# Softmax weights transposed by the tensor engine instead of by DMA, attention in rounds of three steps inside the projection gemm, and a fixed instruction order for the tensor engine in the first phase

## The chip, the cores and the metric

The kernel runs on one core of one Trainium2 chip. The metric is the device time of one execution in microseconds. In the texts PE is TensorE (the matmul engine), PEld its weight loads, DVE is VectorE, ACT is ScalarE, POOL is GpSimd and SP is SyncE, whose queue issues nearly all DMAs.

## The reference, cut to what matters

One layer of a decoder runs on 2048 prompt tokens and on 8 sample rows. The part that the change touches is the attention of the prompt. Its q, k and v come from one projection:

```python
def project_mixers(h, w_in, pos):
    z = h @ w_in                       # 1024 -> 2304 columns
    qa, ka, va, qb, kb, vb = jnp.split(z, points, axis=-1)
    ...
def banded_attention(q, k, v, window): # blocks of 128 queries, keys of the block and of the one before
    s = jnp.einsum('nbqhgd,nbkhd->nbhgqk', qb, kk) * scale
    s = jnp.where(valid[None, :, None, None], s, NEG)
    lse = jax.nn.logsumexp(s, axis=-1)
    p = jnp.exp(s - lse[..., None])
    o = jnp.einsum('nbhgqk,nbkhd->nbqhgd', p.astype(vv.dtype), vv)
...
def dilated_prompt(q, k, v):           # DIL_GROUPS = ((128, 1), (512, 4), (2048, 16))
    for w, d in DIL_GROUPS:
        ... banded_attention(to_res(q)[:, :, :, None], to_res(k), to_res(v), w // d)
    return combine_by_denominator(jnp.stack(outs), jnp.stack(lses), axis=0)
```

After it come the output projection, a cross-attention into 256 memory tokens, and a feed-forward network with a short convolution; all numbers are float32.

## The kernel before, in words

**Two phases.** The first computes the input projection, all the banded attention of the prompt and the keys and values of the memory tokens; the second runs output projection, cross-attention and feed-forward network in four chunks of 512 tokens. The change is in the first phase.

**The projection.** The 2304 columns of `w_in` are nine blocks of 256 (six of them, `COLS_A`, for mixer A, three, `COLS_B`, for mixer B), and the 16 tiles of 128 tokens are four groups. `ORDER` says which blocks of which group follow one another: first the six A blocks of groups 0, 1, 2 and 3, then the three B blocks of groups 3, 0, 1 and 2. For one block and one token tile `gemm_tile` (line 667) makes 24 matmuls of 256 columns: float32 is split into a high and a low part (`wh`, `wl`, `xh`, `xl`), and three products are summed over eight slices of the inner dimension. `evac_in` then turns queries and keys by their angles on DVE (`rope_to`) and stores the rows to DRAM. The last 16 tiles of the phase are those of the memory tokens (`mem_gemm`).

**The attention.** It is cut into 64 jobs (`Job`): 16 each of kinds `d1`, `d4`, `d16` and `b`; each job is a block of 128 queries with eight heads, worked on as two halves of four heads. The texts call a half a quad. There are 128 quads: 84 with two key blocks (the wide ones) and 44 with one (the narrow ones: all of `d16`, and the first blocks of the others). A quad passes three stages. `stage_a` computes the scores on PE into two PSUM banks (`se`, `so`), adds the mask and takes the maximum on DVE (line 556, four instructions), scales the maximum (line 559), and takes four exponentials on ACT (line 561). `stage_b` makes a float16 high part of the weights on ACT (line 569) and a low part on DVE (line 570) and lets one DMA transpose of the SP queue turn both into `pT` (line 572). `stage_c` multiplies with the values on PE (line 585) and copies the result on DVE (line 592). `job_prep` loads nothing: it transposes the job's queries and keys on PE into a bank of the PSUM pair `t` (lines 473 and 482), and ACT and DVE split them into high and low parts.

**What sets the order.** `attn_step` does one third of a round: scores of a quad, then the weights of an earlier quad, then the values of a still earlier one. `filler(n)` is called after every `gemm_tile` and makes two, three or four such steps, in a program order which a scheduler may then change: each engine's instructions are ordered by it at build time, and on the chip every engine works through its list in that order. In the second phase nothing of this changes.

Of the kernel before, what the change touches and what calls it, by code (L numbers as in the profile page):

```python
# [21 lines left out]
NS = 8  # L22
# [4 lines left out]
ST = 528  # L27
# [8 lines left out]
def tile_layer(ctx: ExitStack, tc: tile.TileContext, I, C, O):  # L36
# [32 lines left out]
    mm = nc.tensor.matmul  # L69
# [207 lines left out]
    nc.tensor.transpose(pv[:, 0:120], vrow, ident[:120, :120])  # L277
# [6 lines left out]
    def xprep(key, nxt=None):  # L284
# [3 lines left out]
        def norm():  # L288
            ss = sbL.tile([128, 1], F32, tag="ss", name="ss", bufs=3)
            junk = at_start("sm", 2) if key in range(4) else sbL.tile([128, 1024], F32, tag="xr", name="junk")  # L290
            act(out=junk[:rows], in_=x[:rows], func=ACTF.Square, accum_out=ss[:rows])
            r = sbL.tile([128, 1], F32, tag="r", name="r", bufs=18)
            rms_r(r[:rows], ss[:rows], 1.0 / D, 1, rows)
            rows_r[key] = r

        if key == "s":
            norm()
            pt = bank("t", 2)
            for k in range(8):
                nc.tensor.transpose(pt[:, k * NS:(k + 1) * NS], x[:NS, k * 128:(k + 1) * 128], ident[:NS, :NS])  # L300
# [13 lines left out]
        if key in (1, 2, 3):  # L314
            xr = at_start(*(("p2", 2), ("p2", 2), ("pT", 3))[key - 1]).rearrange("p (k t) -> p k t", k=8)
        else:
            xr = sbL.tile([128, 8, 128], F32, tag="xr", name="xr")
        for hf in range(2):
            pt = bank("t", 2)
            for k in range(4):  # L320
                kk = hf * 4 + k
                nc.tensor.transpose(pt[:, k * 128:(k + 1) * 128], x[:, kk * 128:(kk + 1) * 128], ident)
# [146 lines left out]
    def t_split(ins, hi, lo):  # L469
        pt = bank("t", 2)  # L470
        n = len(ins)
        for i, a in enumerate(ins):
            nc.tensor.transpose(pt[:, i * 128:(i + 1) * 128], a, ident)
# [4 lines left out]
    def t_copy(ins, out, eng="a"):  # L478
        pt = bank("t", 2)
        n = len(ins)  # L480
        for i, a in enumerate(ins):
            nc.tensor.transpose(pt[:, i * 128:(i + 1) * 128], a, ident)
        hi_of(out, pt[:, 0:n * 128].rearrange("p (k t) -> p k t", k=n), eng)

    def job_prep(job):
        job.full = job.kind == "d16" or (job.kind == "d4" and job.t == 0)
        if job.kind == "b":
            job.qh = sbR.tile([128, 4, 128], F32R, tag="qh", name="qh", bufs=2)
            job.ql = sbR.tile([128, 4, 128], F32R, tag="ql", name="ql", bufs=2)
            t_split([job.q[:, 128 * j:128 * j + 128] for j in range(4)], job.qh, job.ql)  # L490
            rh, rl = ring("b")
            s = job.t % 2
            t_split([job.k], rh[:, s], rl[:, s])
            job.kh, job.kl = rh, rl
        else:
            if job.full:
                job.qh = sbR.tile([128, 4, 128], F32, tag="qh", name="qf", bufs=2)
                job.kh = sbR.tile([128, 2, 4, 128], F32, tag="kh", name="kf", bufs=1)
                t_copy([job.q[:, 128 * j:128 * j + 128] for j in range(4)], job.qh)
                t_copy([job.k[:, 128 * j:128 * j + 128] for j in range(4)], job.kh[:, 1], "v")  # L500
                job.slots, job.vs, job.mo = [1], [job.v3], None
                job.ost = sbR.tile([128, ST], F32, tag="ost", name="ost", bufs=5)
# [3 lines left out]
            t_split([job.q[:, 128 * j:128 * j + 128] for j in range(4)], job.qh, job.ql)  # L506
            if job.kind == "d1":
                rh, rl = ring("d1")
                s = job.t % 2
            else:  # L510
                rh = sbR.tile([128, 2, 4, 128], F32R, tag="kh", name="kh", bufs=1)
                rl = sbR.tile([128, 2, 4, 128], F32R, tag="kl", name="kl", bufs=1)
                s = 1
            t_split([job.k[:, 128 * j:128 * j + 128] for j in range(4)], rh[:, s], rl[:, s])
            job.kh, job.kl = rh, rl
            if job.kind == "d4" and job.t > 0:
                t_split([job.kp[:, 128 * j:128 * j + 128] for j in range(4)], rh[:, 0], rl[:, 0])
                vprev["d4"] = job.vp3

        v3 = job.v3  # L520
        first = job.kind == "d16" or job.t == 0
        if first:
            job.slots, job.vs, job.mo = [s], [v3], None
        else:
            pv3 = vprev[job.kind]
            if s == 1:
                job.slots, job.vs, job.mo = [0, 1], [pv3, v3], 0
            else:
                job.slots, job.vs, job.mo = [0, 1], [v3, pv3], 1
        if job.kind in ("d1", "b"):  # L530
            vprev[job.kind] = v3
        job.ost = sbR.tile([128, ST], F32, tag="ost", name="ost", bufs=5)

    def stage_a(job, i):
# [15 lines left out]
        sm = sbR.tile([128, 4, 256], F32, tag="sm", name="sm", bufs=2)  # L550
# [62 lines left out]
    quads = deque()  # L613
    loaded = deque()
    pipe = {"b": None}
    ready = deque([None] * 2)
# [3 lines left out]
    def attn_busy():  # L620
        return bool(jobs or loaded or quads or pipe["b"] or any(ready))

    def attn_step():
        if not attn_busy():
# [1132 lines left out]
```

## Time and profile before

| | us |
|---|---|
| median of 3 runs | 3235.93 |
| lowest and highest run | 3235.06, 3238.74 |
| the profiled execution, its own time | 3230.24 |
| its span, from first to last instruction | 3228.5 |
| first phase, to about | 1000 |
| second phase | about 2228 |

The profiled execution's own time is 1.7 us above its span, and 5.7 us below the median of the runs. The mean granted TensorE clock over the span is 0.984. The first phase ends where the windows stop showing attention, at about 1000 us.

### The profile page before, as it was taken

Reading aid. Unit: us, or ns where it says so; the run is one execution under the profiler, and the core shown is the slowest. Engines: PE = TensorE matmul, PEld = TensorE weight load, DVE = VectorE, ACT = ScalarE, POOL = GpSimd, SP = SyncE. Lnnn points to the kernel's source line nnn. Section 1 sums busy time; section 2 is a strip of 40 time slices with the busy share of each in tenths; the row PEclk is TensorE's granted clock in tenths of the full one; section 3 lists DMA queues with packets and bytes.
Section 4 is the critical chain, followed back from the end, with each engine's and each line's share of the span. In section 5 each row is a group of like instructions: output and inputs, shape, how many; then the busy total and the mean of one; then the engine's idle time right before and its main releaser. Section 6 shows DMA issues by size and latency. Waiting matters only on the chain.

```text
span 3228.5 us, 58044 instructions
## 1 busy us (share of the span) xinstructions
PE 3100.5 (96%) x22290; PEld 2713.9 (84%) x22290; DVE 2147.1 (67%) x4299; ACT 1417.1 (44%) x2793; POOL 1013.7 (31%) x959
## 2 busy tenths in 40 slices
PE   8999989889888999999999999999999999999999
PEld 8998888788877888888887778798877778999998
DVE  7687677787886667665567766555687665554544
ACT  3555654666665444223444333444433343432322
POOL 2711613224244046342205524320554332110102
PEclk9999999998899999999999999999999999999999
DMA  6899999999897346664525555453476445223231
GB/s 211 249 253 237 270 243 230 252 242 220 191 231 230 119 152 209 204 198 162 207 97 184 169 168 183 144 196 111 159 240 235 157 151 179 73 86 96 89 95 64
DMA packets 621837, 580.14 MB, mean 180 GB/s; under 512 B 264140, under 2 KB 554104, under 8 KB 620432
## 3 DMA queue, kind: packets, MB, share of 16 engines
q1 hardware_dynamic: 616808, 572.21, 60.6%
q10 hardware_dynamic: 4608, 4.20, 0.4%
q8 instruction: 175, 2.87, 0.4%
q14 instruction: 102, 0.84, 0.1%
q0 software_dynamic: 144, 0.03, 0.0%
HBM read 457.55 MB, written 136.66 MB: 184 GB/s over the span
## 4 chain that ended last, share of the span: by engine, by line
PE 64%; DVE 7%; DMA 7%; POOL 3%; issue 3%; ACT 2%; SPq 1%; POOLq 0%; DVEq 0%; ACTq 0%
PE g L863 18%; PE g L862 18%; PE g L864 18%; DMA pT<-p 4%; PE s L1358 1%; PE g L1398 1%; PE o L585 1%; DVE wl L120 1%; DVE p L570 1%; DVE sm L556 1%; DMA kx<-in_cache_mem_k_dram 1%; PE g L672 1%; PE g L674 1%; PE g L673 1%; DMA mrg<-o_d 1%
## 5 line engine op out<-in xcount | busy, mean ns | idle before, releaser
L120 DVE TENSOR_TENSOR wl<-wr,wh 128x1024 fp32r<-128x1024 f32 (+1 forms) x406 | 535.7, 1320 | 359.8 <-ACT wh L110 358.3
L110 ACT ACTIVATE wh<-wr 128x1024 fp32r<-128x1024 f32 (+1 forms) x444 | 460.8, 1040 | 674.5 <-PE g L864 382.7
L863 PE MATMUL g<-h,wl 128*128 128x512 f32 (+2 forms) x2080 | 729.5, 351 | 0.0
L862 PE MATMUL g<-h,wh 128*128 128x512 f32 (+2 forms) x2080 | 729.5, 351 | 0.0
L864 PE MATMUL g<-h,wh 128*128 128x512 f32 (+2 forms) x2080 | 725.1, 349 | 0.0
L862 PEld LDWEIGHTS g<-h,wh 128*128 128x128 f32 x2080 | 390.7, 188 | 58.6 <-issue 1.0
L864 PEld LDWEIGHTS g<-h,wh 128*128 128x128 f32 x2080 | 391.2, 188 | 55.2 <-issue 0.5
L863 PEld LDWEIGHTS g<-h,wl 128*128 128x128 f32 x2080 | 390.8, 188 | 54.9 <-issue 1.4
L672 PE MATMUL g<-wh,xh 128*128 128x256 f32 x1152 | 340.4, 296 | 1.1 <-ACT z L383 0.7
L674 PE MATMUL g<-wh,xl 128*128 128x256 f32 x1152 | 333.1, 289 | 0.3 <-DVE xl L120 0.3
L673 PE MATMUL g<-wl,xh 128*128 128x256 f32 x1152 | 331.8, 288 | 0.0
L862 PE MATMUL g<-act,wh 128*128 128x512 f32 (+2 forms) x880 | 310.4, 353 | 8.2 <-ACT act L110 5.7
L863 PE MATMUL g<-act,wl 128*128 128x512 f32 (+2 forms) x880 | 309.4, 352 | 0.0
L864 PE MATMUL g<-act,wh 128*128 128x512 f32 (+2 forms) x880 | 308.0, 351 | 0.0
L561 ACT ACTIVATE sm<-sm,ost 128x256 f32<-128x256 f32 (+1 forms) x512 | 234.8, 460 | 155.1 <-DVE ost L559 154.4
L892 POOL TENSOR_TENSOR sq<-sq 128x512 f32<-128x512 f32 (+1 forms) x83 | 125.2, 1508 | 484.2 <-ACT sq L887 451.3
L672 PEld LDWEIGHTS g<-wh,xh 128*128 128x128 f32 x1152 | 223.5, 194 | 6.4 <-ACT z L383 0.9
L674 PEld LDWEIGHTS g<-wh,xl 128*128 128x128 f32 x1152 | 222.9, 193 | 4.0 <-DVE xl L120 1.2
L673 PEld LDWEIGHTS g<-wl,xh 128*128 128x128 f32 x1152 | 223.3, 194 | 2.1 <-issue 0.2
L862 PE MATMUL g<-oT,wh 128*128 128x512 f32 (+2 forms) x608 | 216.1, 356 | 4.5 <-ACT oT L110 4.5
L863 PE MATMUL g<-oT,wl 128*128 128x512 f32 (+2 forms) x608 | 215.9, 356 | 0.0
L864 PE MATMUL g<-oT,wh 128*128 128x512 f32 (+2 forms) x608 | 211.6, 355 | 0.0
(353 smaller groups left out, 6084.2 us busy)
## 6 DMA issues: line engine op xcount, KB each, us to landing
wr<-in_w_up_dram SPq DMA_DIRECT2D x176, 512.0 KB
wr<-in_w_down_dram SPq DMA_DIRECT2D x80, 512.0 KB
out_dram<-in_cache_a_k_dram SPq DMA_DIRECT2D x32, 1023.5 KB
out_dram<-in_cache_a_v_dram SPq DMA_DIRECT2D x32, 1023.5 KB
wr<-in_w_in_dram SPq DMA_DIRECT2D x60, 512.0 KB
v<-va_d SPq DMA_DIRECT2D x60, 384.0 KB
wr<-in_w_out_dram SPq DMA_DIRECT2D x32, 512.0 KB
wr<-in_w_xq_dram SPq DMA_DIRECT2D x32, 512.0 KB
```

The source lines that it names most:

```text
L110: act(out=out, in_=in_, func=ACTF.Copy)
L120: e.tensor_tensor(out=out, in0=in_, in1=hi.bitcast(F32), op=ALU.subtract)
L556: vec.tensor_tensor_reduce(out=sm[:, x, 0:n], in0=S[e][:, u * n:(u + 1) * n], in1=m_, scale=1.0, scalar=-3e38, op0=ALU.add, op1=ALU.max, a ...
L561: act(out=sm[:, x, 0:n], in_=sm[:, x, 0:n], func=ACTF.Exp, scale=0.125, bias=nb[:, x:x + 1], accum_out=job.ost[:, 520 + 4 * i + x:521 + 4 ...
L570: vec.tensor_tensor(out=p2[:, 1], in0=sm[:, :, 0:n], in1=p2[:, 0], op=ALU.subtract)
L672: mm(p[:, 0:256], h[:, kt, :], wh[:, q, :], start=(kt == 0), stop=False)
L673: mm(p[:, 0:256], h[:, kt, :], wl[:, q, :], start=False, stop=False)
L674: mm(p[:, 0:256], l[:, kt, :], wh[:, q, :], start=False, stop=(kt == 7))
L862: mm(o, wh[:, q, c], pn[:, 0, a:b], start=st, stop=False)
L863: mm(o, wl[:, q, c], pn[:, 0, a:b], start=False, stop=False)
L864: mm(o, wh[:, q, c], pn[:, 1, a:b], start=False, stop=en)
L892: pl.tensor_tensor(out=acc[:, 0:self.ncol], in0=acc[:, 0:self.ncol], in1=sq[:, 0:self.ncol], op=ALU.add)
```

## The change

The change has three parts.

1. `stage_b` no longer makes `p2` and no longer issues a DMA. Each key block of a quad's weights (four heads, 128x128 float32 each) is transposed by four PE instructions into a bank of `t`; ACT copies the bank to the float16 high part and DVE subtracts to get the low part, both straight into `pT`.
2. A round is one `stage_a`, then `stage_c` and `stage_b` together, then a part of `job_prep` of the next job, which now returns a list of pieces (`queries`, `keys`, `before`). `gemm_tile` and `mem_gemm` call `filler(1)` between matmuls of one accumulation, so that the steps of a round stand between pieces of six, nine or twelve matmuls. The number of steps for each tile stays two, three or four. A quad's values follow its weights one round later, not two.
3. All matmuls and transposes of PE go through `mm` and `tr`, which in the first phase fix them to program order (`keep_in_program_order`). The scheduler still orders DVE, ACT, POOL and SP.

`sm` has four buffers, not two, and the first `x` tiles use them.

```diff
-    mm = nc.tensor.matmul
+    in_order = [True]
+
+    def pinned(ins):
+        return tc.keep_in_program_order(ins) if in_order[0] else ins
+
+    def mm(*args, **kw):
+        return pinned(nc.tensor.matmul(*args, **kw))
+
+    def tr(*args):
+        return pinned(nc.tensor.transpose(*args))
...
     def stage_b(job, i, sm):
 
-        n = 128 * len(job.slots)
-        p2 = sbR.tile([128, 2, 4, n], F16, tag="p2", name="p2", bufs=2)
-        act(out=p2[:, 0], in_=sm[:, :, 0:n], func=ACTF.Copy)
-        vec.tensor_tensor(out=p2[:, 1], in0=sm[:, :, 0:n], in1=p2[:, 0], op=ALU.subtract)
-        pT = sbR.tile([128, 16, 128], F16, tag="pT", name="pT", bufs=3)[:, 0:n // 16]
-        nc.sync.dma_start_transpose(out=pT, in_=p2.rearrange("p g x k -> p (g x k)"))
-        v = pT.rearrange("p (g x h) t -> p g h x t", g=2, x=4)
-        return v[:, 0], v[:, 1]
+        nh = len(job.slots)
+        pT = sbR.tile([128, 2, 2, 4, 128], F16, tag="pT", name="pT", bufs=3)
+        for hf in range(nh):
+            pt = bank("t", 2)
+            for x in range(4):
+                tr(pt[:, x * 128:(x + 1) * 128], sm[:, x, hf * 128:(hf + 1) * 128], ident)
+            v = pt.rearrange("p (x t) -> p x t", x=4)
+            act(out=pT[:, 0, hf], in_=v, func=ACTF.Copy)
+            vec.tensor_tensor(out=pT[:, 1, hf], in0=v, in1=pT[:, 0, hf], op=ALU.subtract)
+        return pT[:, 0], pT[:, 1]
...
         elif s == 1:
...
+            if pipe["b"]:
+                stage_c(*pipe["b"])
+            pipe["b"] = None
+            if pipe["a"]:
+                jb, i, sm = pipe["a"]
+                pipe["b"] = (jb, i, *stage_b(jb, i, sm))
+            pipe["a"] = pipe["n"]
         else:
...
+            begin_prep()
+            if cur[0] is not None:
+                if len(to_prep) > 1 and nxt[0] is not None and not hasattr(nxt[0], "qh"):
+                    to_prep.popleft()()
+            else:
+                while to_prep:
+                    to_prep.popleft()()
...
-    def gemm_tile(u, h, l):
+    def gemm_tile(u, h, l, steps=0):
         p = bankA("g")
         for kt in range(8):
             wh, wl = u[kt // 4]
             q = kt % 4
+            if kt * steps // 8 > (kt - 1) * steps // 8 and kt:
+                filler(1)
             mm(p[:, 0:256], h[:, kt, :], wh[:, q, :], start=(kt == 0), stop=False)
...
-                p = gemm_tile(u, *xT[tt])
+                p = gemm_tile(u, *xT[tt], 4 if j in COLS_B else 2 if oi < 3 else 3)
...
-                filler(4 if j in COLS_B else 2 if oi < 3 else 3)
+                filler(1)
```

How the instructions now stand is shown at one place, in the `b` jobs near the end of the projection. These are the rows of PE of the changed kernel: the weights of one quad are transposed from `sm_14140` into both banks of `t`, six matmuls of the projection follow, then the queries of the next job (`raw`) are transposed into `t_14345`, and three more matmuls of the projection follow.

```order
L78 MATMUL t_14323<-ident_81,sm_14140 128x128 x4
L78 MATMUL t_14330<-ident_81,sm_14140 128x128 x4
L75 MATMUL g_14273<-wh56_12755,xh_13108 128x256
L75 MATMUL g_14273<-wl56_12756,xh_13108 128x256
L75 MATMUL g_14273<-wh56_12755,xl_13109 128x256
L75 MATMUL g_14273<-wh56_12755,xh_13108 128x256
L75 MATMUL g_14273<-wl56_12756,xh_13108 128x256
L75 MATMUL g_14273<-wh56_12755,xl_13109 128x256
L78 MATMUL t_14345<-ident_81,raw_13865 128x128 x4
L75 MATMUL g_14273<-wh57_12761,xh_13108 128x256
L75 MATMUL g_14273<-wl57_12762,xh_13108 128x256
L75 MATMUL g_14273<-wh57_12761,xl_13109 128x256
```

Before, `sm` had no reader on PE; `t` has two banks, given out in turn, so `t_14345` is the bank of `t_14323`. After three more matmuls of the projection the scores of the next quad follow (`se_14364`, `so_14365`).

On ACT of the kernel before, a comparable place in the `b` jobs reads so: exponentials of a quad (line 561), its float16 copy (line 569), and the copies of queries and keys from PSUM between them.

```order
L561 ACTIVATE sm_14004,ost_13878<-sm_14004,ost_13878 128x256 x4
L110 ACTIVATE ringb0_12763<-t_14150 128x128
L569 ACTIVATE p2_14155<-sm_14004 128x1024
L561 ACTIVATE sm_14130,ost_13878<-sm_14130,ost_13878 128x256 x4
L598 ACTIVATE es_14540<-es_14540 128x8
L110 ACTIVATE qh_14341<-t_14343 128x512
L569 ACTIVATE p2_14260<-sm_14130 128x1024
L561 ACTIVATE sm_14249,ost_14154<-sm_14249,ost_14154 128x256 x4
```

On ACT of the changed kernel, at the place that PE's rows show, the order is this (`pT` is written from the two banks of `t`, `qh` is the next job's queries):

```order
L570 ACTIVATE sm_14262,ost_14233<-sm_14262,ost_14233 128x256 x4
L583 ACTIVATE pT_14322<-t_14323 128x512
L583 ACTIVATE pT_14322<-t_14330 128x512
L120 ACTIVATE qh_14343<-t_14345 128x512
L570 ACTIVATE sm_14378,ost_14233<-sm_14378,ost_14233 128x256 x4
L583 ACTIVATE pT_14454<-t_14455 128x512
L583 ACTIVATE pT_14454<-t_14462 128x512
```

What moved: the exponentials of a newer quad (`sm_14262`) now stand ahead of the copies out of `t` for an older quad (`sm_14140`, by PE's rows). Counted over ACT's whole list of the changed kernel, this is so for 106 of the 128 quads.

On DVE of the changed kernel, the same place: mask and maximum of the newer quad (line 565, from `se` and `so`), their scale (line 568), the copy of the values' result (line 603), and then the two subtractions out of `t` (line 584) for the older quad and the low part of the queries.

```order
L565 ISA sm_14262,mx_14263<-so_14249,mask_102 128x256
L565 ISA mx_14263 128x1
L568 TENSOR_SCALAR ost_14233<-mx_14263 128x4
L603 COPY ost_13975<-o_14280 128x2x2x64
L584 TENSOR_TENSOR pT_14322<-t_14323,pT_14322 128x512
L584 TENSOR_TENSOR pT_14322<-t_14330,pT_14322 128x512
L130 TENSOR_TENSOR ql_14344<-t_14345,qh_14343 128x512
L565 ISA sm_14378,mx_14379<-se_14364,mask_102 128x256
```

Before, the subtraction (line 570) read `sm` and `p2` in SBUF and held no PSUM bank; now the two of line 584 stand between a quad's maxima and the next quad's.

## Rows read from the trace of the kernel before

**Rows 1.** The page: busy time by engine; the chain of waits by line, 107:1000.

```profile
PE 3100.5 (96%) x22290; PEld 2713.9 (84%) x22290; DVE 2147.1 (67%) x4299; ACT 1417.1 (44%) x2793; POOL 1013.7 (31%) x959
...
by line: DMA pT<-p 13.0%; PE o L585 4.0%; issue 3.7%; DVE p L570 3.3%; DVE sm L556 3.3%; PE g L672 3.0%; PE g L674 2.8%; PE g L673 2.8%; PE se L548 2.6%; PE so L548 1.7%; DVE ost L559 1.3%; ACT sm L561 1.3%; ACT p L569 1.2%; DVE t L363 1.1%
```

**Rows 2.** Windows by stage: length, PE, PEld, DVE, ACT, POOL, clock, DMA share, GB/s.

```profile
107.00:221.20 114.20, 107.76 (x1186) 102.10 (x1185) 89.66 (x273) 67.03 (x185) 45.76 (x52) 0.98 0.98 260
221.20:357.30 136.10, 125.80 (x1486) 118.44 (x1483) 100.87 (x285) 78.60 (x199) 33.36 (x36) 0.95 0.99 249
357.30:501.40 144.10, 130.66 (x1620) 122.14 (x1618) 101.14 (x279) 79.19 (x195) 46.24 (x45) 0.98 1.04 251
501.40:665.30 163.90, 144.68 (x1598) 131.49 (x1597) 131.67 (x481) 97.28 (x324) 57.43 (x52) 0.96 0.98 241
665.30:770.00 104.70, 93.74 (x1140) 85.28 (x1138) 84.61 (x264) 68.24 (x178) 29.33 (x26) 0.92 1.05 234
770.00:875.00 105.00, 95.20 (x1202) 86.22 (x1200) 89.54 (x297) 69.59 (x199) 32.01 (x32) 0.92 0.83 191
875.00:1000.00 125.00, 101.39 (x1338) 92.22 (x1338) 102.24 (x282) 82.93 (x223) 58.71 (x40) 0.95 1.02 243
```

**Rows 3.** Waits from 107 to 1000 us: total, times, longest.

```profile
ACT p L569 <- DMA pT<-p: 54.1, 28, 7.8
...
PE o L585 <- DMA pT<-p: 43.1, 34, 2.8
```

**Rows 4.** DVE by line and shape, 107 to 1000 us: busy us, mean ns.

```profile
L570 DVE TENSOR_TENSOR p<-sm,p 128x1024 f16<-128x1024 f32 x84 | 119.8, 1426 | 36.4 <-ACT p L569 36.1
...
L559 DVE TENSOR_SCALAR ost<-mx 128x4 f32<-128x4 f32 x128 | 39.3, 307 | 0.8
L570 DVE TENSOR_TENSOR p<-sm,p 128x512 f16<-128x512 f32 x44 | 36.8, 837 | 21.6 <-ACT p L569 21.4
L120 DVE TENSOR_TENSOR ql<-t,qh 128x512 fp32r<-128x512 f32 x44 | 29.9, 680 | 2.1 <-ACT qh L110 2.1
L556 DVE CUSTOM_DVE_ANT_0 sm<-so,mask 128x128 f32<-128x128 f32 x88 | 21.9, 282 | 4.4 <-PE so L548 4.4
```

**Rows 5.** ACT by line and shape, 107 to 1000 us: busy us, mean ns.

```profile
L561 ACT ACTIVATE sm<-sm,ost 128x256 f32<-128x256 f32 x336 | 166.4, 497 | 100.8 <-DVE ost L559 100.3
...
L561 ACT ACTIVATE sm<-sm,ost 128x128 f32<-128x128 f32 x176 | 68.4, 390 | 54.3 <-DVE ost L559 54.0
...
L110 ACT ACTIVATE qh<-t 128x512 fp32r<-128x512 f32 x44 | 25.8, 587 | 20.5 <-PE t L473 14.2 <-DMA pT<-p 3.8 <-PE so L548 2.5
```

**Rows 6.** Timeline around 710 us, clock at full level: start us, duration us, what.

```profile
709.86 0.38 PE L548 MATMUL so<-kh,qh 64*128 64x256 f32 x1
...
710.45 0.40 PE L548 MATMUL so<-kh,ql 64*128 64x256 f32 x2
...
711.50 1.34 PE L585 MATMUL o<-v,pT 128*128 128x64 bf16 x40 [0.65 <-DMA pT<-p]
...
712.73 0.41 DVE L556 CUSTOM_DVE_ANT_0 sm<-se,mask 128x256 f32<-128x256 f32 x1
...
712.88 0.28 PE L672 MATMUL g<-wh,xh 128*128 128x256 f32 x1
...
713.00 0.28 PE L673 MATMUL g<-wl,xh 128*128 128x256 f32 x1
...
714.10 0.08 DVE L556 DVE_READ_ACCUMULATOR2_ANT mx<- 128x1 f32 x1
```

**Rows 7.** Timeline of the start: transposes, first projection matmul, load of the sample rows.

```profile
8.34 1.94 PE L322 MATMUL t<-ident,x 128*128 128x128 f32 x8 [1.10 <-DMA x<-in_x_prompt_dram]
...
16.52 0.56 PE L672 MATMUL g<-wh,xh 128*128 128x256 f32 x1
...
21.65 0.42 SPq L259 DMA_DIRECT2D x<-in_x_sample_dram  x1
...
23.13 1.03 PE L322 MATMUL t<-ident,x 128*128 128x128 f32 x8
```

More of the change, by code (lines that the diff above doesn't have):

```diff
@@ L276, in tile_layer @@
     pv = bankA("pv")
-    nc.tensor.transpose(pv[:, 0:120], vrow, ident[:120, :120])
+    tr(pv[:, 0:120], vrow, ident[:120, :120])
     vec.tensor_copy(out=vecs, in_=pv[:, 0:120])
@@ L289, in norm @@
             ss = sbL.tile([128, 1], F32, tag="ss", name="ss", bufs=3)
-            junk = at_start("sm", 2) if key in range(4) else sbL.tile([128, 1024], F32, tag="xr", name="junk")
+            junk = at_start("sm", 4) if key in range(4) else sbL.tile([128, 1024], F32, tag="xr", name="junk")
             act(out=junk[:rows], in_=x[:rows], func=ACTF.Square, accum_out=ss[:rows])
@@ L472, in t_split @@
         for i, a in enumerate(ins):
-            nc.tensor.transpose(pt[:, i * 128:(i + 1) * 128], a, ident)
+            tr(pt[:, i * 128:(i + 1) * 128], a, ident)
         v = pt[:, 0:n * 128].rearrange("p (k t) -> p k t", k=n)
@@ L481, in t_copy @@
         for i, a in enumerate(ins):
-            nc.tensor.transpose(pt[:, i * 128:(i + 1) * 128], a, ident)
+            tr(pt[:, i * 128:(i + 1) * 128], a, ident)
         hi_of(out, pt[:, 0:n * 128].rearrange("p (k t) -> p k t", k=n), eng)
@@ L486, in job_prep, with queries @@
         job.full = job.kind == "d16" or (job.kind == "d4" and job.t == 0)
[L487 to L495, printed above, removed]
+        cols = [slice(128 * j, 128 * j + 128) for j in range(4)]
+        def queries():
             if job.full:
                 job.qh = sbR.tile([128, 4, 128], F32, tag="qh", name="qf", bufs=2)
[L498 to L502, printed above, removed]
+                t_copy([job.q[:, c] for c in cols], job.qh)
                 return
@@ L505, in job_prep @@
             job.ql = sbR.tile([128, 4, 128], F32R, tag="ql", name="ql", bufs=2)
[L506 to L509, printed above, removed]
-            else:
[L511 to L529, printed above, removed]
@@ L534, in stage_a, with before @@
+        def before():
+            t_split([job.kp[:, c] for c in cols], job.kh[:, 0], job.kl[:, 0])
+        return [queries, keys] + ([before] if job.kind == "d4" and job.t > 0 else [])
     def stage_a(job, i):
@@ L612, in tile_layer @@
     jobs = deque()
-    quads = deque()
     loaded = deque()
-    pipe = {"b": None}
-    ready = deque([None] * 2)
+    to_prep = deque()
+    cur = [None, 0]
+    nxt = [None]
+    pipe = {"a": None, "b": None}
     sub = [0]
@@ L620, in attn_busy, with attn_left, fetch, begin_prep @@
     def attn_busy():
-        return bool(jobs or loaded or quads or pipe["b"] or any(ready))
+        return bool(jobs or loaded or to_prep or nxt[0] or cur[0] or pipe["a"] or pipe["b"])
+    def attn_left():
+        return [*jobs, *loaded] + [j for j in (nxt[0], cur[0]) if j]
+    def fetch():
+        while len(loaded) < 2 and jobs:
+            jb = jobs.popleft()
+            job_load(jb)
+            loaded.append(jb)
+    def begin_prep():
+        if nxt[0] is None and loaded:
+            nxt[0] = loaded.popleft()
+            to_prep.extend(job_prep(nxt[0]))
     def attn_step():
@@ L697, in mem_prep @@
         if t == 0:
-            while any(jb.kind != "b" for jb in [*jobs, *loaded, *(q[0] for q in quads)]):
+            while any(jb.kind != "b" for jb in attn_left()):
                 filler(1)
```

103 lines of the change are left out of this document (58 added, 45 removed).

## The prediction

> **What bounds the kernel now.** I read the page first. PE is busy for 96% of the span [rows 1], but that mixes two phases. In the windows by stage [rows 2] the second phase is absent because nothing in it changes; the first phase, from 107 to 1000 us, has PE at 81% to 94% busy, and the granted clock at 0.92 to 0.98, so some stretches ran at 1.2 GHz. DVE is at 70% to 85%, and the DMA share is about 1.0 in six of the seven stages: the queue is full. The chain of waits of this stretch says what the fullness costs: 13% of it, some 116 of 893 us, is the landing of the transposed weights `pT`, more than any engine's line has [rows 1]. The waits say who stands still for it: ACT 54 us before it may reuse `p2`, PE 43 us before the values [rows 3]. So the first phase is held by a transfer, and PE and DVE both have time to spare in it.
>
> **What goes.** All 128 DMA transposes, with their waits. Also the DVE subtractions of line 570, 119.8 + 36.8 = 157 us [rows 4]. These waits cannot be subtracted as they stand, since what follows them may wait for something else. That is what has to be worked out.
>
> **What comes on PE.** 84 wide quads have two key blocks and 44 have one, each block is four transposes: (168 + 44) x 4 = 848. Eight transposes took 1.03 us at full clock and 1.94 at half [rows 7]; without the drain of the last that is 0.11 us each, so 94 us at full clock. PE's idle time in the seven stages is 893 - 799 = 94 us, and low clock hides more, so they fit only if they fall into idle time.
>
> **What comes on DVE and ACT.** 212 subtractions from PSUM, of the shape that `ql` has (0.68 us, [rows 4]): 144 us, 12 less than before. 212 copies out of PSUM like that of `qh` (0.59 us, [rows 5]) take about what the old float16 copies took. Neither engine gets fuller.
>
> **A round, by occupancy of PE.** Line 672's matmuls start 0.12 us apart [rows 6]. A round with four steps to a tile has 18 of them: 2.2 us. Twelve scores run in pairs, 6 x 0.12 = 0.7. Values 1.2 (1.34 with its drain, [rows 6]). Weights 0.9, queries or keys 0.45. Some seven changes of operand kind at 0.09, by estimate, 0.6. Sum 6.0 us. With three steps to a tile 6.7, with two 8.15.
>
> **A round, by what waits for what.** Here the pinned order matters. `t` has two banks. In the rows of order, the weights take both, so the queries or keys of the same round need the first one back, and on PE everything behind them stands still: six matmuls and the next quad's scores. The bank comes back after its copy on ACT and its subtraction on DVE. On ACT that copy stands behind the four exponentials of the newer quad (106 of 128 quads). Those need that quad's maxima, and those its scores, which are this round's first step. So the round closes on itself: scores, from the first start to the last end 709.86 to 710.85, 0.99 [rows 6]; mask and maximum 712.73 to 714.18, 1.45 [rows 6]; scale 0.31 [rows 4]; exponentials 4 x 0.497 and a last read, 2.05 [rows 5]; copy 0.59 [rows 5]; subtraction 0.68 [rows 4]; four transposes 0.44; six matmuls 0.72; changes of operand kind 0.2; seven hand-overs between engines, 0.3 by estimate. Sum **7.7 us**, against 6.0 of occupancy. With three and two steps to a tile the piece before the scores is longer: 8.1 and 8.45. Behind a transpose of keys the scores also wait for the low half (copy 0.59 and subtraction 0.68 against about 1.2 us of cover); with the two transposes of a `d4` job that is more, on average 0.35 us a round for `d1` and `d4`.
>
> Narrow quads use one bank, so the loop through `t` opens. Their line on DVE and ACT is shorter, four maxima of 0.28, scale 0.31, four exponentials of 0.39, copy, subtraction, 4.3 us with overlap; occupancy is 4.55. Every second round the keys' copy (0.68, as `ql`) and the scores come behind it: 5.65. Mean 5.1.
>
> **The sum, by stage of [rows 2].** Rounds by the program's loops, after against before:
> 107 to 221: 10 narrow rounds x 6.7 (occupancy with two steps), 6 x 8.45, 32 transposes of `x` 3.5: 121 against 114, +7.
> 221 to 357: 16 x 8.8 + 3.5 = 144 against 136, +8.
> 357 to 501: 16 x 8.45, then some 162 matmuls without attention, 20: 155 against 144, +11.
> 501 to 665: 32 x 5.1 + 6 for the sample rows = 169 against 164, +5.
> 665 to 770: 16 x 8.05 = 129 against 105, +24.
> 770 to 875 (`b`, keys are one transpose): 16 x 7.6 = 121 against 105, +16.
> 875 to 1000: 16 x 7.6, 96 matmuls alone 11.5, merge 7: 140 against 125, +15.
> That is +86. The start: PE's first projection matmul, at 16.52, now stands behind the transposes of the sample rows, whose load was issued at 21.65 [rows 7]; that is 10 us later at most, and part of it is caught up because transposes are then behind it: +6 (bounds 0 and 14). Turning instructions stand between maxima and scale at about 71 places of DVE's new list, at about 0.3 us: +20 (bounds 0, if they fill a wait, and 40). In 22 of 128 quads ACT takes the copy first, about 0.6 us gained each: -14. In all **+98**, so a span of 3228.5 + 98 = 3326. The profiled execution's own time, 3230.24, is 5.7 under the median of 3235.93, and the span 7.4: **3334 us**. The seven hand-overs and the changes of kind are the widest estimates: at nothing the loop is 7.2, at double 8.2, 84 wide rounds x 0.5 = 42 either way. Own range 3280 to 3385.
>
> **Rivals.** *PE sets the pace (faster).* The loop does not close, because copies come earlier on the chip than in my hand-worked round, and each wide round takes its occupancy: 120 + 134 + 127 + 152 + 98 + 93 + 111 = 835 (the last two with 5.8 a round, since a `b` job's keys are one transpose) against 893, -58; with +6 for the start and some 6 of remaining stalls, 3190. For it: all of the 116 us of landing leave the chain. Against: the orders of PE, ACT and DVE above leave no other way round. It decides as soon as a wide round falls under some 6.6 us, which is what the stage 665 to 770 takes now (105 us for 16).
>
> The Trainium skill, page VectorE: DVE Perf Modes, section The three transpose paths, speaks for this rival: it gives 390 ns for a 128x128 transpose on TensorE and 1309 ns for the DMA's, in 2-byte numbers. The trace agrees that PE's are far cheaper (0.11 us apart against a chain of landings), but the page says nothing of what queues behind a PSUM bank.
>
> *The loop half closes.* Where the matmul pieces of other lengths let ACT run ahead, half the rounds take the loop and half occupancy: (98 - 46) / 2, about +26, 3262. Slower still.
>
> *Dear transposes.* If transposes let the clock fall, they cost 1.94 us for eight, twice as much [rows 7]: 848 x 0.11 = 93 us more, of which those of the weights stand under the exponentials and those in the loop, half of the rounds' PE part with them, do not: +60 on top, 3394. For it: the clock is already at 0.92 in two stages whose PE has gaps [rows 2]; against: it is 0.95 to 0.98 in the three stages to 501 us, which transpose `q` and `k` too and most of them also `x`.
>
> The Trainium skill, page TensorE: Matmul & The Clock Gate, Part 4: PE-mode transpose, speaks against the change in this way: it measured about 275 ns in one kernel's context, and says that transposes do not count as activity for the clock. By 275 ns the 848 would be 233 us, not 94. The trace disagrees on the price: eight in 1.03 us [rows 7].
>
> *It does not do what it says.* Landing of other transfers, not of `pT`, could be what fills the queue; the loads of `q`, `k` and values then keep the first phase at its length: 3236. Against: `pT` alone is named in both waits [rows 3].
>
> **Chances.** Loop as worked out 0.60, half closed 0.10, dear transposes 0.06, PE sets the pace 0.19, no change 0.05. So slower by over 0.2% 0.75, within 0.2% (6.5 us, about what a measurement of this kernel can tell from no change) 0.05, faster 0.20. The range for 8 in 10 leaves out the upper half of the dear transposes and a little over half of the fast case: 3195 to 3395.
>
> **What would show it.** In the profile after: no DMA transposes and a DMA share well under 1.0; 848 new PE instructions at about 0.11 us; wide rounds 7.5 to 8.5 us apart (start of scores to start of scores) with PE waiting for the DVE subtraction before the transposes of queries and keys, and ACT's copy out of `t` waiting not for PE but behind exponentials; first phase ending near 1100. I am wrong if wide rounds come at 6.6 us or less, or if PE's longest waits there are for something else than the bank.

## The result and the profile after

The changed kernel takes 3431.0 us (median of 4 runs, 3426.2 to 3435.6) against 3235.5 of the kernel before: a ratio of 1.0607, 95% interval 1.0584 to 1.063, some 195 us slower. The direction was forecast, the size was twice the forecast +98, and the time lies outside the range. The profiled execution has a span of 3428.0 us.

The page first, its line of PE and its line of the DMA share in 40 slices:

```profile
PE 3198.8 (93%) x23138; PEld 2799.2 (82%) x23138; DVE 2156.7 (63%) x4383; ACT 1427.8 (42%) x2877; POOL 976.7 (28%) x959
...
DMA  6755554664324353566463555545366545232331
```

848 instructions of PE are new, as counted, and the DMA share is near one half where it was full. Next the windows by stage, which answer to [rows 2]; the stages end where the projection's matmuls of the same stage end (us, PE, PEld, DVE, ACT, POOL, clock, DMA share, GB/s):

```profile
118.70:259.70 141.00, 123.13 (x1319) 115.48 (x1317) 93.06 (x285) 69.95 (x199) 35.86 (x46) 0.96 0.59 180
259.70:420.70 161.00, 139.01 (x1606) 128.83 (x1605) 110.44 (x300) 81.94 (x212) 29.31 (x36) 0.97 0.54 157
420.70:579.60 158.90, 138.47 (x1708) 128.35 (x1707) 97.76 (x287) 77.14 (x204) 36.19 (x44) 0.99 0.53 160
579.60:670.20 90.60, 76.05 (x825) 69.60 (x825) 61.78 (x235) 45.86 (x155) 23.57 (x19) 0.91 0.58 171
670.20:761.10 90.90, 82.17 (x914) 75.27 (x913) 68.95 (x256) 49.26 (x168) 32.79 (x34) 0.95 0.66 190
761.10:896.20 135.10, 105.00 (x1285) 94.04 (x1284) 87.63 (x273) 69.69 (x194) 23.03 (x23) 0.94 0.43 124
896.20:1033.00 136.80, 103.07 (x1259) 93.72 (x1257) 88.63 (x296) 67.12 (x205) 29.05 (x36) 0.88 0.30 90
1033.00:1195.00 162.00, 128.44 (x1498) 116.69 (x1496) 100.01 (x311) 88.97 (x247) 49.51 (x39) 0.88 0.38 120
...
118.70:1195.00 1076.30, 895.35 (x10397) 821.96 (x10395) 708.25 (x2237) 549.93 (x1581) 259.31 (x274) 0.94 0.49 146
```

The last line is all the stages in one window. The first phase ends at 1195, not 1100. No engine is full in these stages: PE is at 75% to 90%, DVE at 62% to 76%, DMA at 0.66 or less. In all PE is busy for 895 us and idle for 181; before, by the lines of [rows 2], it was busy for 799 and idle for 94. So of the 183 us by which these stages grew, 96 are work of PE, about what 848 transposes at 0.11 us come to, and 87 are idle time. Such a picture is one of waits, so the waits of PE come next (118 to 1195 us: us in total, times, longest):

```profile
PE t L78 <- DVE pT L584: 83.4, 58, 4.0
PE t L78 <- issue: 20.9, 13, 2.3
PE t L78 <- ACT mz L1657: 12.0, 8, 5.2
PE t L78 <- DMA srow<-in_state_conv_dram: 11.2, 1, 11.2
PE t L78 <- DMA raw<-qa_d: 8.4, 1, 8.4
PE se L75 <- DVE ringd L130: 7.9, 7, 2.2
PE t L78 <- ACT xr L333: 7.4, 5, 3.6
...
PE se L75 <- DVE kf L124: 7.1, 7, 2.8
```

The longest is the one forecast: transposes (line 78) that wait for DVE's subtraction of the weights (line 584) to return the bank. Around it stands a list of waits for other things: all rows of this view add up to 179 us, and 83 of them are the bank's. The 13 waits for which the profile names no releaser (`issue`, 20.9 us) stand at the same place, before transposes of the next job's `raw`, and may be the bank's too. The timeline shows one wide round with that wait, and ahead of it a wait of PE and two pairs of matmuls, one at either clock (start us, us, what):

```profile
801.08 0.71 PE L78 MATMUL t<-ident,raw 128*128 128x128 f32 x4 [2.26 <-issue]
...
801.81 0.42 PE L75 MATMUL g<-wl,xh 128*128 128x256 f32 x1
802.02 0.41 PE L75 MATMUL g<-wh,xl 128*128 128x256 f32 x1
...
803.01 0.58 PE L75 MATMUL se<-ringd,qh 64*128 64x256 f32 x1
...
808.10 0.28 PE L75 MATMUL g<-wl,xh 128*128 128x256 f32 x1
808.22 0.28 PE L75 MATMUL g<-wh,xl 128*128 128x256 f32 x1
...
811.75 0.38 PE L75 MATMUL se<-kh,qh 64*128 64x256 f32 x1
...
819.86 0.38 PE L75 MATMUL se<-kh,qh 64*128 64x256 f32 x1
...
820.88 0.42 DVE L565 CUSTOM_DVE_ANT_0 sm<-se,mask 128x256 f32<-128x256 f32 x1 [0.29 <-PE so L75]
...
822.26 0.42 DVE L367 TENSOR_TENSOR t<-g,cr 128x256 f32<-128x256 f32 x1
822.60 0.48 DVE L373 TENSOR_TENSOR t<-g,cr 128x128 f32<-128x128 f32 x2
...
822.77 1.07 PE L78 MATMUL t<-ident,sm 128*128 128x128 f32 x8
...
822.99 0.16 DVE L568 TENSOR_SCALAR ost<-mx 128x4 f32<-128x4 f32 x1
...
823.19 0.51 ACT L570 ACTIVATE sm<-sm,ost 128x256 f32<-128x256 f32 x1 [3.32 <-DVE ost L568]
...
823.60 0.36 PE L75 MATMUL g<-wh,xh 128*128 128x256 f32 x1
...
825.18 1.06 ACT L583 ACTIVATE pT<-t 128x512 f16<-128x512 f32 x2
825.79 1.29 DVE L584 TENSOR_TENSOR pT<-t,pT 128x512 f16<-128x512 f32 x2 [1.98 <-ACT pT L583]
...
826.54 0.66 PE L78 MATMUL t<-ident,raw 128*128 128x128 f32 x4 [1.99 <-DVE pT L584]
...
827.88 0.38 PE L75 MATMUL se<-ringd,qh 64*128 64x256 f32 x1
```

Read from the scores at 819.86: maxima from 820.88, two turning instructions (lines 367 and 373) before the scale at 822.99, exponentials from 823.19, the older quad's copy only behind them at 825.18, subtraction 825.79, and then the bank is free and PE, idle for 1.99 us, transposes the next queries; next scores at 827.88. The round is 8.02 us, in the forecast's order of pieces.

### The profile page after: what moved, and what is told of

It reads as the page before. It is cut to its first block, busy times and chain, and to the rows that moved or that the text cites. A ratio compares the mean times of both kernels' runs of the same rounds, so it can differ in the third digit from the quotient of the medians.

```text
span 3428.0 us, 59536 instructions
## 1 busy us (share of the span) xinstructions
PE 3198.8 (93%) x23138; PEld 2799.2 (82%) x23138; DVE 2156.7 (63%) x4383; ACT 1427.8 (42%) x2877; POOL 976.7 (28%) x959
## 5 line engine op out<-in xcount | busy, mean ns | idle before, releaser
L75 PE MATMUL g<-h,wh 128*128 128x512 f32 (+2 forms) x4160 | 1094.1, 350 | 2.2 <-DVE gt L1501 1.6
L75 PEld LDWEIGHTS g<-h,wh 128*128 128x128 f32 x4160 | 725.6, 188 | 117.2 <-issue 2.4
L75 PE MATMUL g<-act,wh 128*128 128x512 f32 (+2 forms) x1760 | 467.8, 352 | 7.8 <-ACT act L120 3.8
L75 PE MATMUL g<-wh,xh 128*128 128x256 f32 x1152 | 364.4, 316 | 0.3 <-DVE t L373 0.2
L75 PEld LDWEIGHTS g<-act,wh 128*128 128x128 f32 x1760 | 309.1, 189 | 57.3 <-ACT act L120 4.2
L75 PE MATMUL g<-oT,wh 128*128 128x512 f32 (+2 forms) x1216 | 328.3, 355 | 0.8 <-ACT oT L120 0.8
L75 PEld LDWEIGHTS g<-oT,wh 128*128 128x128 f32 x1216 | 213.0, 188 | 33.9 <-ACT oT L120 1.0
L130 POOL TENSOR_TENSOR wl<-wr,wh 128x1024 fp32r<-128x1024 f32 x38 | 91.0, 2393 | 509.0 <-ACT wh L120 509.0
L584 DVE TENSOR_TENSOR pT<-t,pT 128x512 f16<-128x512 f32 x212 | 141.0, 685 | 99.8 <-ACT pT L583 99.0
```

Of the source, the lines that this page charges most:

```text
L75: return pinned(nc.tensor.matmul(*args, **kw))
L130: e.tensor_tensor(out=out, in0=in_, in1=hi.bitcast(F32), op=ALU.subtract)
L584: vec.tensor_tensor(out=pT[:, 1, hf], in0=v, in1=pT[:, 0, hf], op=ALU.subtract)
```

## The experiments

Eight kernels, before and after among them, split the change into its parts (medians in us, from the runs below; where `t` has three banks, `o` has one in place of two):

| | not pinned | pinned |
|---|---|---|
| DMA transposes, old rounds | 3233 (before) | 3310 |
| PE transposes, old rounds | 3265 | 3370 |
| PE transposes, new rounds, `t` of three banks | 3257 | 3371 |
| PE transposes, new rounds, `t` of two banks | 3332 | 3431 (after) |

**A third bank for the loop.** `t` gets three banks, `o` one; PE's order is unchanged.

```diff
-            pt = bank("t", 2)
+            pt = bank("t", 3)          # every place
-        po = bank("o", 2)
+        po = bank("o", 1)
```

> The changed kernel with a third bank for `t`, taken from `o` (2 to 1); PE's order stays as it is. Three theories for the +195 us over the kernel before. Bank loop: the pinned PE stands before the transposes of queries and keys until DVE's subtraction returns the bank (83 us of waits in the profile after); with a third bank these waits go and some of the low-clock time of the gaps with them: 3340 to 3380 us, wide rounds near 6.5 us. Late producers in general: the wait only moves to the next late thing (exponentials before the weights' transposes, one bank of `o` before the values): 3400 to 3440. Price of the transposes (848 at 0.11 us, PE full): no change, within 10 us of 3431.

Measured 3371.0 us (ratio to before 1.0405, 1.0378 to 1.0432): 60 us less. The waits of PE, 118 to 1140 us:

```profile
PE se L75 <- ACT ringb L120: 21.2, 11, 3.3
PE t L78 <- DVE pT L584: 15.8, 10, 3.8
PE se L75 <- DVE ringd L130: 12.0, 13, 2.3
PE se L75 <- ACT ringd L120: 11.6, 11, 2.0
```

The bank's wait falls from 83.4 to 15.8 us, a fall of 68; 60 us are gained at the end, and the waits for late keys (`ringb`, `ringd`) have grown. The loop is real, and it is under a third of the 195 us. The Trainium skill, page Perfetto Trace Analysis, section Optimization Strategy, says that the same gap repeating on the engine that should be saturated can mean too little PSUM for the next tile; the trace agrees, with a bank that gives back 60 us.

**The copies ahead of the exponentials.** The other cure of the same loop, two banks kept.

```diff
-        for x in range(4):
-            act(out=sm[:, x, 0:n], ..., func=ACTF.Exp, ...)
-        return sm
+        def exps():
+            for x in range(4):
+                tc.keep_in_program_order(act(out=sm[:, x, 0:n], ..., func=ACTF.Exp, ...))
+        return sm, exps
...
                 pipe["b"] = (jb, i, *stage_b(jb, i, sm))
+            while pend:
+                pend.popleft()()
```

> The changed kernel with ACT's copies of a quad's weights put ahead of the exponentials of the newer quad (the exponentials are issued one step later, pinned on ACT); two banks of `t`. Bank loop: the copy comes 2.05 us earlier than the end of the exponentials, the waits before the transposes of queries and keys have a mean of 1.4 us, so nearly all of the 83 us go: 3345 to 3385. Late producers: the exponentials now end later and the next round's transposes of the weights wait for them: 3400 to 3450. Price of the transposes: within 10 us of 3431.

3374.6 us (1.0415, 1.0383 to 1.0448): 56 us less, as the bank loop says. **Both cures together:**

> The changed kernel with both cures of the loop, the third bank and the copies ahead of the newer exponentials. If the loop is one thing with two cures, they do not add: 3335 to 3375, like each alone (3371 and 3375). If each removes a wait of its own: 3300 to 3325.

3367.6 us (1.0403, 1.0374 to 1.0432). They do not add: one loop, opened at either place.

**No pins.** `in_order = [True]` becomes `[False]`.

> The changed kernel, nothing pinned on TensorE (the scheduler's order in phase one, as in the kernel before). Bank loop: the scheduler puts matmuls into the waits, 83 us and the transposes' gaps are filled: 3330 to 3370. Late producers: all waits of the pinned order, 180 us by the profile, are filled: 3260 to 3310. Price of the transposes: 3400 to 3440, since the work stays.

3332.3 us (1.0285, 1.026 to 1.0309): 99 us less, in the loop's range. I read this as the scheduler filling the loop; a later run (no pins and three banks) showed that reading wrong.

**Twice the transposes of the weights.**

```diff
-            for x in range(4):
+            for x in [0, 1, 2, 3] * 2:
                 tr(pt[:, x * 128:(x + 1) * 128], sm[:, x, hf * 128:(hf + 1) * 128], ident)
```

> The changed kernel with every transpose of the weights issued twice into the same place (848 more, 94 us by the 0.11 us that they stand apart). Bank loop: in the 84 wide rounds they lie under exponentials for which PE waits anyway, 1.4 us a round against 0.9 us of extra work; the 44 narrow ones pay 0.44 us each, 19 us: 3445 to 3475. Price of the transposes, and late producers too: the whole 94 us, 3515 to 3535; more, if the clock falls with more transposes.

3454.5 us (1.0663, 1.0638 to 1.0688): 848 more transposes add 23 us, 0.03 us each. The bank's wait shrinks as they fill it (118 to 1225 us):

```profile
PE t L78 <- DVE pT L584: 49.5, 39, 4.4
```

So PE has room for most of them in this kernel, since it waits there anyway. What the first 848 cost a PE that has little idle time, the next run shows.

**Part one alone: weights by PE in the kernel before.** `stage_b` is that of the change; `sm` has four buffers, `p2` is gone; rounds and order are those of before.

> The kernel before, with the weights transposed by TensorE and nothing else of the change (old rounds behind whole tiles, nothing pinned; four buffers of `sm` in place of two and two of `p2`). If the landing of the weights was what held the first phase, as I read it in rows 1 and 3: 3130 to 3190. If 848 transposes at 0.11 us come on PE's path whole and the landings' waits only change their name: 3300 to 3335, as the changed kernel without its pins (3332). If the new rounds, not the transposes, make that kernel slow: 3225 to 3270.

3265.4 us (1.0094, 1.0062 to 1.0127), 32 us slower than before. My reading that the landing held the first phase fails: the landings are gone and the time is longer. Three of its windows and the whole phase, columns as above:

```profile
221.00:360.00 139.00, 137.12 (x1583) 128.86 (x1583) 101.05 (x290) 78.35 (x201) 29.40 (x36) 1.00 0.61 182
360.00:505.00 145.00, 142.75 (x1706) 133.25 (x1705) 108.23 (x302) 87.29 (x230) 40.58 (x46) 1.00 0.59 180
...
665.00:770.00 105.00, 102.61 (x1206) 95.23 (x1204) 84.32 (x269) 65.11 (x183) 36.12 (x27) 1.00 0.62 180
...
107.00:1030.00 923.00, 892.20 (x10419) 828.00 (x10418) 702.09 (x2240) 552.78 (x1582) 270.56 (x282) 0.99 0.57 173
```

PE is busy for 98% in the three, at full clock. Over the phase its idle time falls from 94 to 31 us, but it is busy for 892 us in place of 799: 63 us of gaps are won and 93 us of work paid, which is the loss. The three windows shown are about as long as before; the 30 us come behind 770 us (260 us there, against 230 in [rows 2]). And it is 67 us faster than the changed kernel without pins, so the new rounds cost too.

**Pins alone.** The kernel before with its PE instructions pinned in phase one, as the change pins them.

> The kernel before with TensorE pinned to the program in phase one and nothing else of the change: DMA transposes and the old rounds stay. If pinning costs by itself, whatever is waited for, about what taking the pins off gave back in the changed kernel (99 us): 3310 to 3360. If only the loop through `t` makes the pins dear (there is none here, the weights take no bank): 3225 to 3270. If the landings of the weights now stand in PE's way (5 to 11 us each): above 3400.

3309.9 us (1.0224, 1.0193 to 1.0255), 76 us more, at the lower edge of "pins cost by themselves": no weights take a bank here.

**Turned weights and pins, old rounds.**

> The kernel before with turned weights and with pins, without the new rounds. If the pins cost what they cost elsewhere (76 us on the kernel before, 99 on the changed one): 3340 to 3365. If the new rounds are what makes pins bearable (weights, then the wait for their copies, with nothing between): above 3431. If the loop through `t` needs the new rounds' order to close: below 3330.

3370.3 us (1.0421, 1.0402 to 1.0441): 105 us more than without pins, 5 above the first range. It equals the changed kernel with three banks (3371).

**No pins, steps behind whole tiles.** `gemm_tile` is called without steps, and `filler` behind the tile as before.

> The changed kernel without pins, and with the attention's steps behind whole tiles again, as in the kernel before; the new rounds (values, then weights, in one step; queries and keys a step ahead) stay. It splits the 67 us between the kernel before with turned weights (3265) and the changed kernel without pins (3332). If the cutting of tiles into pieces makes the difference (matmuls of the projection run ahead and leave an end of attention alone, with gaps and low clock): 3260 to 3285. If the new rounds do (one round less between weights and values): 3315 to 3345.

3322.5 us (1.0279, 1.0256 to 1.0302): 10 us of the 67 at most come from cutting the tiles; the rounds themselves cost the rest.

**No pins and three banks.**

> The changed kernel without pins and with the third bank of `t`. If the loop through `t` is what the new rounds cost, with pins or without: 3260 to 3285, as the kernel before with turned weights (3265). If without pins the scheduler already fills the loop, and the 57 to 67 us are something else (matmuls that run ahead and leave the attention's end alone): 3315 to 3340.

3256.8 us (1.0071, 1.0055 to 1.0087), 3 us under the first range. The third bank gives back 75 us without pins too, and the kernel is then no slower than the old rounds (3265): the loop is the price of the new rounds, and the scheduler had not filled it. The old rounds with a third bank were not run; their profile names 6.4 us of waits of PE for the bank in all (3.9, 1.6 and 0.9), so there is little for it to win there. The first phase without pins, from 107 us on, first with two banks:

```profile
107.00:1095.00 988.00, 916.07 (x10400) 840.58 (x10398) 697.63 (x2238) 550.10 (x1582) 270.90 (x281) 0.96 0.54 161
```

and with three:

```profile
107.00:1026.00 919.00, 887.08 (x10415) 819.56 (x10416) 705.13 (x2240) 545.41 (x1582) 273.01 (x282) 0.99 0.57 174
```

PE goes from 93% busy at a clock of 0.96 to 97% at 0.99. The waits for the bank that the profile with two banks names are only 14.5 us, so the 75 are not that row alone. With two banks the projection's last matmul starts at 797 us and the last matmul with the values at 1094, with three at 808 and 1023: the time is won where no matmul of the projection is left to stand in the gaps. That this is the reason was not tested.

**Late things out of the way.** The transposes of the convolution's state rows come two column blocks later, those of the memory's keys one step later.

```diff
+                turn = evac_mem(j, t, mem_gemm(u, *MEM[t][:2]), MEM[t][2])
                 filler(1)
+                if turn:
+                    turn()
+                if j == 1 and t == 0:
+                    turn_srow()
```

> The changed kernel with two late things taken out of PE's way: the transposes of the convolution's state rows come two column blocks later in the memory's stage, those of the memory's keys one step later. If the waits that my sum lacked count by what the profile shows (11.2 us and 12.0 us): 3405 to 3417. If they are swallowed by the next wait of the loop: 3425 to 3437.

3412.8 us (1.0547, 1.0518 to 1.0577): 18 us less. The 11.2 us wait for the state rows is gone from the waits, the memory keys' fell from 12.0 to 1.4 us, and the bank's rose (118 to 1178 us):

```profile
PE t L78 <- DVE pT L584: 91.8, 62, 3.6
...
PE t L78 <- ACT mz L1660: 1.4, 1, 1.4
```

22 us of waits are taken away and 8 given to the loop; 18 show at the end. **All cures under pins** (both of the loop, and the late things):

> The changed kernel, pinned, with the third bank, the copies ahead of the exponentials, and the two late transposes moved. If the terms add (64 for the loop, 18 for the late things): 3342 to 3358. If the late things are only seen because the loop is there: 3362 to 3372.

3356.0 us (1.0368, 1.0347 to 1.039): in the range of terms that add, though of the 18 us for the late things 12 show here (3367.6 to 3356.0, and the intervals overlap). About 120 us over before remain.

**The projection's matmuls free of their pins, three banks.** In `gemm_tile` and `mem_gemm`, `mm` becomes the unpinned call; attention and transposes stay pinned.

> The changed kernel with the third bank of `t`, pinned but for the matmuls of the projection and the memory's gemm, which the scheduler may place earlier. If the pins cost because these matmuls may not pass an attention instruction that waits: 3257 to 3300, most of the 114 us that pins cost there. If the attention's own order, transposes of `x` and the start are what waits: 3335 to 3371.

3281.2 us (1.0147, 1.0122 to 1.0172): 90 of the pins' 114 us come back. PE's longest waits, 107 to 1190 us:

```profile
PE o L75 <- DVE pT L584: 12.8, 21, 1.9
PE o L75 <- ACT pT L583: 10.3, 12, 2.1
PE se L75 <- DVE kf L124: 7.5, 7, 3.2
```

The waits for `ringb` and `ringd`, 44.8 us in the three rows shown for three banks and all pins, have left the head of the list (2.3 us for `ringb` remain). So most of the price of the pins is this: a late key, or anything late, holds matmuls that need nothing of it. Some 11 of the 90 us may be the start, where the first projection matmul stands at 16.46 us in place of 27.92. The other 24 us of the pins were not divided.

**The start without pins.** Pins begin with the attention's first step.

> The changed kernel with pins from the attention's first step on only; the start is left to the scheduler. If the later start (first projection matmul at 26.7 in place of 16.5) passes on to the end whole: 3416 to 3425. If the stages behind it absorb it, or the scheduler's start brings nothing once pins follow: 3426 to 3436.

3419.4 us (1.0576, 1.0552 to 1.0601): 12 us less. The two intervals overlap, but the traces agree: the first projection matmul starts at 16.58 us in place of 26.71, the last matmul with the values at 1169 in place of 1185. The start, 10 us later with pins, passes to the end whole.

**Half by PE, half by DMA.** Since PE is full with all weights and DMA with none, the kernel before (no pins, old rounds) with every second quad's weights on PE.

```diff
+        quad[0] += 1
+        if quad[0] % 2:
+            return stage_b_pe(job, i, sm)
         p2 = sbR.tile([128, 2, 4, n], F16, tag="p2", name="p2", bufs=1)
```

> The kernel before, unpinned, with every second quad's weights turned by TensorE (424 transposes) and the others by DMA, three buffers of `sm` and one of `p2`. In the kernel before, the DMA queue is full and PE has gaps; with all quads on PE, PE is full (98% busy). If the two bounds trade, half and half is under both: 3195 to 3230. If each transfer that stays still costs its landing, or one buffer of `p2` does: 3240 to 3265.

3237.0 us in 10 runs, 1.0006 (0.999 to 1.0022): no difference from before. Its first phase in one window:

```profile
107.00:1000.00 893.00, 843.51 (x9988) 780.18 (x9987) 691.17 (x2198) 543.58 (x1540) 285.38 (x282) 0.98 0.78 209
```

PE is busy for 44 us more than before and idle for 44 us less: the 424 transposes went into idle time, and no time was won. With two buffers of `p2` and of `sm`:

> The kernel before, unpinned, with every second quad's weights turned by TensorE, and two buffers of `sm` and two of `p2`, as the kernel before has them. If the one buffer of `p2` held the first half-and-half kernel (3237): 3200 to 3225. If `sm`, which the transposes of TensorE hold a round longer, becomes the wait: 3240 to 3280. If neither: 3232 to 3242.

3237.2 us, 1.0013 (1.0000 to 1.0026): the buffers are not its limit. With every fourth quad on PE, and with three of four:

> As the kernel with every second quad on TensorE, but with every fourth (212 transposes, 23 us of PE). If the two bounds trade: 3200 to 3230. If landings still cost or one buffer of `p2` does: 3240 to 3270.

> As the first half-and-half kernel, with three of four quads on TensorE. If PE is what bounds from there on (70 us of transposes against 47): 3245 to 3265. If what is left of the landings still costs: 3215 to 3235.

Every fourth is 3294.4 us (1.0195, 1.0161 to 1.0228), outside both ranges; ACT waits for the transfer before it may write the one `p2` again (107 to 1066 us):

```profile
ACT p L587 <- DMA pT<-p: 129.2, 51, 7.5
```

where it waited 54.1 with two [rows 3]; that the buffer makes the whole of it was not tried. Three of four are 3248.4 us (1.0045, 1.0029 to 1.006), PE's range. None beats the kernel before.

## Why the prediction was wrong

**What held.** The loop, its place and its order: PE waits longest for DVE's subtraction ahead of the transposes of queries and keys, ACT's copies stand behind exponentials, wide rounds come 8.74, 8.11 and 8.02 us apart where shown (scores at 803.01, 811.75, 819.86, 827.88), the forecast being 7.5 to 8.5 with 8.05 for this stage; the fifteen rounds from 763.90 to 892.50 have a mean of 8.57 and lie between 6.13 and 11.14. Cures at two places give back 60 and 56 us. The transposes are at the forecast 0.11 us or under (eight between 822.77 and the next matmul at 823.60), the turning instructions do stand between maxima and scale. The change of operand kind, an estimate of 0.09, is 0.09 where the scores follow the projection's matmuls (0.21 from 819.65 to 819.86, against 0.12). Copies and subtractions cost what was taken, 0.59 and 0.68 (by line and shape, 118.7 to 1195 us: busy us, mean ns):

```profile
L583 ACT ACTIVATE pT<-t 128x512 f16<-128x512 f32 x212 | 115.8, 582 | 38.5 <-PE t L78 38.3
...
L584 DVE TENSOR_TENSOR pT<-t,pT 128x512 f16<-128x512 f32 x212 | 141.0, 685 | 99.8 <-ACT pT L583 99.0
```

The prices of the pieces of a wide round are right; their sum over the phase is not.

**The step that failed** is "A round, by what waits for what", and with it the stage sums. It priced one undisturbed pass through the loop, then took every round to be that pass, and gave pins no price outside it but +6 for the start and 0.35 us for keys. By stage, measured against forecast: 141 against 121, 161 against 144, 159 against 155, 181.5 against 169 (the two from 580 to 761), 135 against 129, 137 against 121, 162 against 140. The stage of wide rounds with nothing late beside them, 761 to 896, is 6 us off. From 896 to 1033 the wait for the state rows is 11.2 of the 16, in the last stage the memory's keys are 12.0 of the 22, from 580 to 761 one wait for a load of `raw` is 8.4 of the 12.5. The first two stages, 20 and 17 off, hold 25.4 us of waits for other things than the bank (7.4 for `x`, most of the rest late keys and waits without a named releaser); but rounds without turns of `x` also come 9.64 and 9.56 apart there (scores at 275.52, 285.16, 294.72), where 8.8 was priced, so late work is not all of it. Pinned, PE stands for each wait. The start cost 12, not 6.

**Two errors cancel.** In the prediction's own terms the seven stages are 835 us of PE's work (the sum of the rival in which PE sets the pace) and 144 us that the closed loop adds, 979 in all. Measured are about 1076: 895 busy, 83 of waits for the bank (104 with the waits without a releaser), 96 of other waits (75 without those). So the work was 60 us too low and the loop 40 to 61 too dear; that these nearly make up for each other is luck, and what is left of the miss is the waits that had no term. The work could have been read from [rows 2]: 799 us of busy PE and 94 of transposes are 893, not 835.

By the runs the change divides so: without pins and with the loop opened 3257, that is 24 over before; pins 114 on top of that (90 for the projection's matmuls that may not pass a waiting instruction); the loop through two banks 60 on top of that: 198, the whole of the table (195 beside its own runs of before). In the other order the pins are 99 (3431 to 3332) and the loop 75 (3332 to 3257). Either way pins are the largest part, and the forecast's term for them was small.

**The clock** was left out of the sums too. They use full-clock distances of 0.12 us; in the last two stages the granted clock is 0.88, where [rows 2] have 0.92 and 0.95, and the pair at 801.81, behind 2.26 us of idle PE, starts 0.21 apart (the lower level, 1.2 GHz), that at 808.10 0.12. The low stretches lie among gaps; without pins or loop it is 0.95 to 1.00. What the clock alone costs was not isolated. A rough estimate from the busy times: the same work keeps PE busy for 895 us here, at a mean clock of 0.94, and for 887 without pins or loop, at 0.99, so the low stretches lie mostly in time in which PE waits anyway (without pins but with the loop it is 916 at 0.96, which shows how rough this is).

**The premise** in the part on what bounds the kernel also failed: 13% of the chain for the landing, 116 us, is not what its removal brings. Part one alone won 63 us of PE's idle time, paid 93 for the transposes, and lost 32.

**Rivals.** PE sets the pace, 3190: opened and unpinned it does, 97% busy, and it takes 3257 to 3265, so even that price was 67 us or more too low: 887 to 892 us of work in place of 835, and some 31 of idle time where 6 were left for stalls. Dear transposes: refuted, 23 us for 848 more, and the mean granted clock of that kernel's profiled execution is 0.981, against 0.975. The half-closed loop is out by its time, 3262, but not wholly as a mechanism: the bank's wait shows 58 times for 84 wide rounds. No change: out. (The chances of the slower cases add up to 0.76, where 0.75 is stated; nothing hangs on it.)

**Open.** What holds the 49 us in which PE still idles with half and half, at a DMA share of 0.78; what makes up the 24 us of the pins that do not come from the projection's matmuls; and what the clock costs by itself.

## What to carry to other kernels

Pinning an engine to the program turns every late producer of any operand into a stop of that engine: price it by leaving the order free for the long independent work and by listing all waits, not the one loop. When a step borrows a buffer pair that others use, give it one more buffer, or let what frees it go first; here a PSUM bank was worth 60 to 75 us and the order 56. A share of the chain of waits is no measure of the gain: ask what fills the gaps once they close, here 93 us of transposes. And before pricing a loop, add the busy time that is there to the work that comes: no order of that work came under the sum here (893 us; 919 at the least).

## What the hardware showed beyond that

Transposes of float32 on PE are cheap in a row: eight in 1.07 us with the drain of the last, close to the 1.03 of [rows 7], and doubling 848 of them costs 23 us in a kernel whose PE waits at those places. In the kernel with part one alone, PE at 98% busy had a granted clock of 1.00 through whole stages of 139 and 145 us, where the same stages of the kernel before, with gaps, had 0.95 and 0.98 [rows 2].
